# 68 tensor sums and products move from GpSimd (POOL) to VectorE (DVE) in a two-block network on one core

## The chip, the cores and the metric

One core of a Trainium2 chip runs the whole program. The metric is device time in microseconds (us) for one execution. The core has TensorE (PE), which multiplies matrices from SBUF into PSUM, three engines for everything elementwise, VectorE (DVE), ScalarE (ACT) and GpSimd (POOL), and DMA queues that are fed mainly from SyncE (SP) and, for a few small transfers, from POOL. SBUF is the on-chip memory that all engines read and write, PSUM the one into which PE accumulates. An engine takes its own instructions in order and waits on semaphores for those of others.

## The reference

The input is one sequence of 256 tokens with 1024 channels, and it passes through two blocks of two layers each.

```python
# first block, layer 0
z = modulate(rmsnorm(x)) @ w_in
x = x + gt1 * concat(hyena_mixer(z), neighborhood_attention(q, k, v, k_ctx, v_ctx, rpb)) @ w_mix_out
x = x + gt2 * swiglu(modulate(rmsnorm(x)))
# layer 1
x = x + gt1 * fourier_mix(modulate(rmsnorm(x))) @ w_fourier
x = x + gt2 * moe_swiglu(...)          # 8 experts, the best 2 of each token
# second block, layer 0
x = x + g1 * retention_mixer(h, pos)   # q and k are rotated by cos and sin of the position
x = x + g2 * conv_ffn(h)
# layer 1
x = x + g1 * s5_mixer(h)               # a complex linear recurrence over the tokens
x = x + g2 * conv_ffn(h)
return rms_norm(x) * final_norm_g
```

The recurrence of the S5 mixer is s(l) = a * s(l-1) + bu(l), with complex a for each of 64 groups and 64 states, and y = Re(C s) + d * u. Matmuls are computed in nearly full fp32 precision: each weight and each activation is split into a high part (a copy in a rounded format) and a low part (the rest), and the products high x high, high x low and low x high are summed.

## The kernel before, in words

The program is written as a sequence of stages ("segments"): the mixer's input projection with the hyena filters, the attention with its output projection, the feed-forward, the Fourier mixer with the routing, the experts, retention, the first convolutional feed-forward (conv 0), S5, conv 1 and the final norm. Within a segment, calls such as `V.tensor_mul` (DVE), `A.activation` (ACT), `G.tensor_add` (POOL) and `S.matmuls` (PE) are only recorded (class `Sched`, `record`). At the end of a segment `flush` puts them in order by list scheduling: it keeps a clock for each engine, gives each operation a cost by `cost` (a POOL sum or product of n elements a partition 0.15 + 0.0021 n us, one on DVE 0.07 + 0.00104 n us), and issues next what can start first. The order on each engine is therefore made by this planner and is redone within each segment when an operation changes its engine. Nothing moves from one segment to another.

All non-matmul instructions come from one line of the recorder, L364 in the profile, and all matmuls from L376, so the profile is read by the names of tiles. The names that matter:

- `wh`, `wl`: the high part (ACT) and the low part (DVE) of a weight tile `w`, made as weights arrive; PE needs both. `hh`/`hl`, `gh`/`gl`, `mwh` are the same for activations and expert weights.
- `w<-w,cb`: a conditioning product (ada), a row sum on DVE over a 128x1024 weight tile; `mods` collects them.
- Hyena filters (`filters`): spectra `K`, 128x512. To the first two pieces of each spectrum the skip vector is added on POOL.
- Attention (`bias`): a bias tile is loaded by DMA through the tensor `Rd`, and the mask is added to it on POOL (`bias<-bias,bias`, 128x1024). DVE then adds a part of it to the scores in PSUM (`ps_sc<-ps_sc,bias`), takes the row maximum (`nm`), and makes a diagonal matrix `dg` of the reciprocal sums, with which PE scales and transposes the probabilities.
- Routing (`route`): DVE finds the best two experts and the slots of each token in a long chain of small instructions, up to the selection matrix `oh` which PE multiplies by the tokens `tok`. `tok` has a high part (ACT) and a low part (POOL).
- Retention (`rotate`): `rqk` is raw * cos (DVE), `rt` is raw * sin (POOL), and DVE combines both.
- S5 constants (`s5_products`, `cmul`): twelve complex-product pieces 128x512 (`s5aB`, `t`, `s5C`) on POOL, issued during conv 0, and four products `s5dd` (32x256) ahead of the loop.
- S5 loop (`s5`): eight chunks of 4 state tiles. For each chunk ACT makes sine and cosine (`sc`) of the phases in `s5f`, writes the decay factors over `s5f`, and spreads the input over `s5um`; PE makes `ps_bu` (two tiles of 128x512). DVE multiplies these by cosine and sine (`a`, `b`: four products that read PSUM), POOL adds them in two instructions (`a<-a,b`), DVE scans both halves along the tokens (`a<-s5f,a`, a tensor_tensor_scan), and four products turn the state back: two on DVE (`a<-a,sc`, `b<-a,sc`) and two on POOL (`a<-a,sc`, `b<-a,sc`). PE reduces them to `ps_y`, ACT copies that into `s5f`. Behind the last chunk the gated output projection (glu) begins: `s5g` is its input, `yn` the gelu.

The loop's elementwise buffers (`pw.tile`) rotate, so ACT's `sc` of a later chunk waits until the last product of an earlier one has read the buffer.

Of the kernel before, what the change touches and what calls it, by code (L numbers as in the profile page):

```python
# [9 lines left out]
F32 = mybir.dt.float32  # L10
# [3 lines left out]
OP = mybir.AluOpType  # L14
# [5 lines left out]
L = 256  # L20
# [281 lines left out]
class Sched:  # L302
    XLAT = 0.08

    def __init__(self, tc):
        self.tc, nc = tc, tc.nc
        self.direct = False
        self.bw = 360e3
        self.ops = []
        self.V = Queue(self, "DVE", nc.vector)  # L310
        self.A = Queue(self, "ACT", nc.scalar)
        self.G = Queue(self, "POOL", nc.gpsimd)
        self.T = Queue(self, "PE", nc.tensor)
        self.Q = Queue(self, "SP", nc.sync)
        self.table = None
        self.lead = 0
# [69 lines left out]
    def add(self, op, ins, outs):  # L386
        op.idx = len(self.ops)
        op.key = (op.idx - self.lead, op.idx)
        deps = {}
        op.bufs = []  # L390
        for w, vs in ((False, ins), (True, outs)):
            for v in vs:
                if not isinstance(v, View):
                    continue
                b = v.buf
                s = (0, 128, 0, 4096) if b.psum else v.span()
                keep = []
                for (o, s2, w2) in b.log:
                    hit = s[0] < s2[1] and s2[0] < s[1] and s[2] < s2[3] and s2[2] < s[3]
                    if hit and (w or w2) and o is not op:  # L400
                        deps[o.idx] = o
                    covered = w and s[0] <= s2[0] and s2[1] <= s[1] and s[2] <= s2[2] and s2[3] <= s[3]
                    if not (covered and o is not op):
                        keep.append((o, s2, w2))
                keep.append((op, s, w))
                b.log = keep
                if b not in op.bufs:
                    op.bufs.append(b)
        op.deps = list(deps.values())
        self.ops.append(op)  # L410

    def flush(self):
# [146 lines left out]
class Net:  # L559
# [337 lines left out]
    def filters(self, p, x8, x8b, dp):  # L897

        V, A = self.V, self.A
# [10 lines left out]
        dec, skip = ds[:, 0], ds[:, 1]  # L910
# [20 lines left out]
        for o in range(2):  # L931
# [24 lines left out]
            for fch in range(4):  # L956
                ps = self.ps("hy")
                src = S if fch < 2 else Df
                self.mg(ps, [(self.dft[:, tck, fch * 128:fch * 128 + 128], src[:, tck]) for tck in range(2)])
                V.tensor_mul(K[:, fch], ps, rec)  # L960
                if fch < 2:
                    self.G.tensor_add(K[:, fch], K[:, fch], skip[:, o])
                V.memset(K[0:1, 2], 0.0)
            ps = self.ps("hy")
            self.mg(ps[0:1, :], [(self.dft[:, tck, 256:257], S[:, tck]) for tck in range(2)])
# [138 lines left out]
    def bias(self, t, hc4, c, mask):  # L1104
        o = 2048 * hc4 + 128 * c
        self.Q.dma_start(t, self.Rd.raw(lambda v: bass.AP(tensor=v.tensor, offset=v.offset + o,
                                                          ap=[[1, 128], [512, 4], [1, L]])))
        self.G.tensor_tensor(t, t, mask[:, c:c + 1].bcast(4, L), OP.add)
        return t

    def stack_heads(self, t, d, hc4, parts):
# [569 lines left out]
    def route(self, pr):  # L1681
# [114 lines left out]
        V.tensor_tensor(eq, oh[1], pw[:, :, 2:3].bcast(2, NE), OP.mult)  # L1796
        V.tensor_add(gate, gate, eq)
        pick(slice(0, 6))
        tk = pr.tile([128, 2, 2, 512], F32, name="rT", tag="fyh")
        for t in range(2):  # L1800
            for q in range(2):
                s, v = slice(q * 512, q * 512 + 512), tk[:, t, q]
                V.scalar_tensor_tensor(v, turned[2 * t + q], r[:, t:t + 1], bt[:, q], op0=OP.mult, op1=OP.add)
                A.activation(mo["tok"][:, 0, t, s], v, AF.Copy)
                self.G.tensor_sub(mo["tok"][:, 1, t, s], v, mo["tok"][:, 0, t, s].bitcast(F32))

    def gather(self, x, tags):
        mo, V = self.mo, self.V
# [75 lines left out]
    def retention(self):  # L1884
        I, V, A, G = self.I, self.V, self.A, self.G
        with self.segment("ret", dict(mm=4, st=1, o=2, tp=1), pools=(1, 2)) as (p, po):
# [9 lines left out]
            def rotate(c, ps):  # L1896
# [5 lines left out]
                if c % 2:  # L1902
                    d = qk[t][:, j]
                    t1 = po.tile([128, 2, L], F32, name="rt1", tag="rb")
                    V.tensor_mul(d, raw, cn.fold(1, L).bcast(2, L))
                    G.tensor_mul(t1, raw, sn.fold(1, L).bcast(2, L))
                    V.tensor_sub(d[:, 0], d[:, 0], t1[:, 1])
                    V.tensor_add(d[:, 1], d[:, 1], t1[:, 0])

# [157 lines left out]
    def s5_products(self, p):  # L2067
# [2 lines left out]
        self.Q.dma_start(B, self.I["s5_bc"][:, 0:2])  # L2070
        self.Q.dma_start(C, self.I["s5_bc"][:, 2:4])
        t = p.tile([128, 2, 32, 16], F32, name="t5")
        self.cmul(self.G, t, aB, B, (ar, ai))
        self.cmul(self.G, t, C, C, (fr, fi))
        self.s5BC = B, C, aB

    def s5_fill(self, n=1):
# [11 lines left out]
    def s5(self):  # L2089
# [8 lines left out]
        with self.segment("s5", dict(mm=2, bu=4, y=2), pools=(1, 2)) as (p, pw):  # L2098
# [27 lines left out]
            DB, DD = [p.tile([128, 8, 32], F32, name=n) for n in ("s5db", "s5dd")]  # L2126
            quads = [slice(32 * q, 32 * q + 32) for q in range(4)]
            for q in range(4):
                G.tensor_tensor(DD[quads[q]], self.ident[quads[q], quads[q]].fold(1, 32).bcast(8, 32),
                                dsk[quads[q]].fold(8, 1).bcast(8, 32), OP.mult)  # L2130
            for c2 in range(4):
                ps = self.ps("bu")
# [19 lines left out]
            for c in range(8):  # L2152
# [28 lines left out]
                for r in range(2):  # L2181
                    V.tensor_mul(a1[:, r], bu[r].fold(4, H), sc[:, 1])
                    V.tensor_mul(b1[:, r], bu[r].fold(4, H), sc[:, 0])
                G.tensor_add(w[:, 0], a1[:, 0], b1[:, 1])
                G.tensor_sub(w[:, 1], a1[:, 1], b1[:, 0])
                for r in range(2):
                    V.tensor_tensor_scan(w[:, r].fold(4 * H), f4.fold(4 * H), w[:, r].fold(4 * H), 0.0, OP.mult, OP.add)
                a2 = pw.tile([128, 2, 4, H], F32, name="a25")
                V.tensor_mul(a2[:, 0], w[:, 0], sc[:, 1])
                G.tensor_mul(a2[:, 1], w[:, 1], sc[:, 1])  # L2190
                V.scalar_tensor_tensor(b2[:, 1], w[:, 1], -1.0, sc[:, 0], op0=OP.mult, op1=OP.mult)
                G.tensor_mul(b2[:, 0], w[:, 0], sc[:, 0])
                py = self.ps("y")
                terms = ((0, a2, 0), (0, b2, 1), (1, b2, 0), (1, a2, 1))
                self.S.matmuls([(py[quads[q], H:2 * H], DD[:, c], um[:, 1, q], True, False) for q in range(4)]
# [81 lines left out]
```

## Time and profile before

| | |
|---|---|
| three runs | 2335.9, 2336.37 and 2342.92 us, median 2336.37 |
| the profiled execution | 2340.57 us, its span (first to last instruction) 2338.8 |
| ACT busy | 981.6 us (42%), 1722 instructions |
| POOL busy | 135.3 us (6%), 116 instructions |
| DMA | 651.66 MB, mean 279 GB/s |
| mean granted TensorE clock | 0.966 |

The busy shares are means over stages that are limited by different engines. POOL's sums and products stand in six places: the filters and the first bias tiles (up to 195 us), attention (195 to 262), routing (around 572), rotation (1542 to 1590), S5 constants (1790 to 1812) and the S5 stage (1970 to 2072). A stage is read from its own window: an engine that is busy for nearly all of a window while the others wait for it is what that window costs. Two neighbouring instructions of DVE overlap a little in the records (the next starts some 0.08 us before the end of the one before), so a sum of durations is slightly more than the time that they take in a row.

### The profile page before, as it was taken

The numbers are of one execution on the slowest core, as the hardware profiler recorded it, in microseconds if no ns is written. First come the engines' busy times: TensorE is split into PE (matmuls) and PEld (weight loads), VectorE is DVE, ScalarE is ACT, GpSimd is POOL, SyncE is SP. The second block draws the span as 40 slices with busy tenths as digits, with TensorE's granted clock in tenths as the row PEclk, the third lists the DMA queues.
The fourth block names the chain that finished last, engine by engine and source line by source line (L and its number), as shares of the span: only waits on it lengthen the run. The fifth ranks groups of instructions, "written<-read, shape, count | busy, mean of one in ns | idle before, by whom it ended". The sixth has DMA issues, their size and how long they took to land. (4 is left out here: it accounts for less than half of the span.)

```text
span 2338.8 us, 40671 instructions
## 1 busy us (share of the span) xinstructions
PE 2189.4 (94%) x16402; PEld 1599.2 (68%) x16402; DVE 1504.7 (64%) x2734; ACT 981.6 (42%) x1722; POOL 135.3 (6%) x116
## 2 busy tenths in 40 slices
PE   7998999986999999999999999899998998779998
PEld 4787889976544444454444444389998998468997
DVE  6886889875433343454444444388969998968864
ACT  4434654453222332232323332153656756436553
POOL 0013000000000000000000000010003001520000
PEclk9998999998999999999999999899999999889999
DMA  8577379965599999988989999638645685115742
GB/s 305 186 248 189 136 299 360 323 239 223 223 391 388 399 401 420 408 327 359 420 332 419 398 420 420 238 127 327 252 178 218 222 294 225 71 56 188 262 160 93
DMA packets 103868, 651.66 MB, mean 279 GB/s; under 512 B 14087, under 2 KB 20520, under 8 KB 31160
## 3 DMA queue, kind: packets, MB, share of 16 engines
q1 hardware_dynamic: 100216, 644.26, 71.2%
q0 software_dynamic: 3456, 4.72, 1.2%
q8 instruction: 131, 2.15, 0.4%
q14 instruction: 65, 0.53, 0.1%
HBM read 644.71 MB, written 4.23 MB: 277 GB/s over the span
## 5 line engine op out<-in xcount | busy, mean ns | idle before, releaser
L364 DVE TENSOR_TENSOR wl<-w,wh 128x1024 fp32r<-128x1024 f32 (+1 forms) x356 | 399.0, 1141 | 69.4 <-ACT wh L364 69.1
L376 PE MATMUL ps_mm<-hh,wh 128*128 128x256 f32 (+1 forms) x1472 | 430.8, 293 | 11.3 <-ACT hh L364 5.6
L364 ACT ACTIVATE wh<-w 128x1024 fp32r<-128x1024 f32 (+1 forms) x356 | 338.3, 979 | 236.7 <-PE ps_mm L376 173.2
L376 PE MATMUL ps_mm<-hl,wh 128*128 128x256 f32 (+1 forms) x1472 | 422.0, 287 | 5.8 <-DVE hl L364 5.7
L376 PE MATMUL ps_mm<-hh,wl 128*128 128x256 f32 (+1 forms) x1472 | 420.0, 285 | 5.5 <-DVE wl L364 5.5
L376 PE MATMUL ps_a<-w,xg 128*32 128x256 f32 (+1 forms) x3136 | 367.9, 452 | 3.9 <-DMA w<-in_moe_w 2.4
L364 DVE TENSOR_TENSOR mwh<-w,mwh 128x512 fp32r<-128x512 f32 x336 | 226.2, 689 | 124.2 <-ACT mwh L364 71.5
L364 ACT ACTIVATE mwh<-w 128x512 fp32r<-128x512 f32 x336 | 206.6, 629 | 233.3 <-PE ps_h L376 181.2
L376 PEld LDWEIGHTS ps_mm<-hh,wh 128*128 128x128 f32 x1472 | 283.1, 192 | 21.4 <-ACT hh L364 7.9
L376 PEld LDWEIGHTS ps_mm<-hl,wh 128*128 128x128 f32 x1472 | 283.3, 192 | 10.9 <-DVE hl L364 8.6
L376 PEld LDWEIGHTS ps_mm<-hh,wl 128*128 128x128 f32 x1472 | 284.2, 193 | 6.5 <-DVE wl L364 6.4
L376 PEld LDWEIGHTS ps_a<-w,xg 128*32 128x32 f32 (+1 forms) x3136 | 115.3, 118 | 160.5 <-issue 119.1
L364 DVE SCALAR_TENSOR_TENSOR w<-w,cb 128x1024 f32<-128x1024 f32 x176 | 213.4, 1233 | 6.2 <-DMA w<-in_ada_w 5.8
L376 PE MATMUL ps_h<-mwh,xs 128*128 128x512 f32 x672 | 192.9, 416 | 0.0
L376 PE MATMUL ps_a<-w,gt 128*32 128x256 f32 (+1 forms) x1568 | 183.7, 450 | 8.4 <-DVE gt L364 8.4
L376 PEld LDWEIGHTS ps_h<-mwh,xs 128*128 128x128 f32 x672 | 116.1, 189 | 61.4 <-issue 36.2
L364 ACT ACTIVATE gg<-ps_a 64x256 f32<-64x256 f32 (+1 forms) x63 | 29.8, 473 | 288.2 <-PE ps_a L376 288.2
L376 PE MATMUL ps_mm<-gh,wh 128*128 128x256 f32 x528 | 149.4, 283 | 0.0
L376 PE MATMUL ps_mm<-gh,wl 128*128 128x256 f32 x528 | 148.8, 282 | 0.2 <-DVE wl L364 0.2
L376 PE MATMUL ps_mm<-gl,wh 128*128 128x256 f32 x528 | 148.5, 281 | 0.0
L376 PEld LDWEIGHTS ps_a<-w,gt 128*32 128x32 f32 (+1 forms) x1568 | 58.4, 117 | 102.3 <-issue 63.1
L364 DVE TENSOR_TENSOR gg<-gg,ps_a 64x256 f32<-64x256 f32 (+1 forms) x63 | 33.8, 537 | 107.7 <-ACT gg L364 107.1
(454 smaller groups left out, 3491.9 us busy)
## 6 DMA issues: line engine op xcount, KB each, us to landing
w<-in_moe_w SPq DMA_DIRECT2D x336, 1024.0 KB, 10.9
w<-in_ada_w SPq DMA_DIRECT2D x88, 1024.0 KB, 6.9
w<-in_cf_up SPq DMA_DIRECT2D x44, 1024.0 KB, 5.0
w<-in_ret_in SPq DMA_DIRECT2D x24, 1024.0 KB, 4.9
w<-in_ffn_up SPq DMA_DIRECT2D x22, 1024.0 KB, 7.1
w<-in_cf_dn SPq DMA_DIRECT2D x32, 704.0 KB, 5.3
w<-in_w_in SPq DMA_DIRECT2D x12, 1024.0 KB, 7.3
w<-in_ffn_dn SPq DMA_DIRECT2D x16, 704.0 KB, 5.7
```

Source lines behind the costliest of these rows:

```text
L364: op.fn = lambda: getattr(obj, m)(*[_real(a) for a in args], **{k: _real(v) for k, v in kw.items()})
L376: mm(_real(o), _real(a), _real(b), start=st, stop=sp, skip_group_check=True)
```

## The change

Every sum, difference and product on tensors that POOL did is given to DVE, unchanged in shape and operands: 4 additions to `K`, 8 bias sums, 4 low parts of `tok`, 8 rotation products, 12 pieces of the S5 constants, 4 products `s5dd` and, in the S5 loop, 32 (16 sums, 8 + 8 products). POOL keeps its memsets and its DMAs. For the low parts of `tok` the planner also gets a dependency (`behind`), so that they are issued behind the first part of the routing's chain.

```diff
@@ Sched
+        self.behind = []
...
-        op.deps = list(deps.values())
+        op.deps = list(deps.values()) + [o for o in self.behind if o.idx not in deps]
@@ filters
                 if fch < 2:
-                    self.G.tensor_add(K[:, fch], K[:, fch], skip[:, o])
+                    V.tensor_add(K[:, fch], K[:, fch], skip[:, o])
@@ bias
-        self.G.tensor_tensor(t, t, mask[:, c:c + 1].bcast(4, L), OP.add)
+        self.V.tensor_tensor(t, t, mask[:, c:c + 1].bcast(4, L), OP.add)
@@ route
         pick(slice(0, 6))
+        last = [o for o in self.S.ops if o.eng == "DVE"][-1:]
...
                 A.activation(mo["tok"][:, 0, t, s], v, AF.Copy)
-                self.G.tensor_sub(mo["tok"][:, 1, t, s], v, mo["tok"][:, 0, t, s].bitcast(F32))
+                self.S.behind = last
+                V.tensor_sub(mo["tok"][:, 1, t, s], v, mo["tok"][:, 0, t, s].bitcast(F32))
+                self.S.behind = []
@@ rotate
                     V.tensor_mul(d, raw, cn.fold(1, L).bcast(2, L))
-                    G.tensor_mul(t1, raw, sn.fold(1, L).bcast(2, L))
+                    V.tensor_mul(t1, raw, sn.fold(1, L).bcast(2, L))
@@ s5_products
-        self.cmul(self.G, t, aB, B, (ar, ai))
-        self.cmul(self.G, t, C, C, (fr, fi))
+        self.cmul(self.V, t, aB, B, (ar, ai))
+        self.cmul(self.V, t, C, C, (fr, fi))
@@ s5
             for q in range(4):
-                G.tensor_tensor(DD[quads[q]], ...
+                V.tensor_tensor(DD[quads[q]], ...
...
                 for r in range(2):
                     V.tensor_mul(a1[:, r], bu[r].fold(4, H), sc[:, 1])
                     V.tensor_mul(b1[:, r], bu[r].fold(4, H), sc[:, 0])
-                G.tensor_add(w[:, 0], a1[:, 0], b1[:, 1])
-                G.tensor_sub(w[:, 1], a1[:, 1], b1[:, 0])
+                V.tensor_add(w[:, 0], a1[:, 0], b1[:, 1])
+                V.tensor_sub(w[:, 1], a1[:, 1], b1[:, 0])
...
                 V.tensor_mul(a2[:, 0], w[:, 0], sc[:, 1])
-                G.tensor_mul(a2[:, 1], w[:, 1], sc[:, 1])
+                V.tensor_mul(a2[:, 1], w[:, 1], sc[:, 1])
                 V.scalar_tensor_tensor(b2[:, 1], w[:, 1], -1.0, sc[:, 0], op0=OP.mult, op1=OP.mult)
-                G.tensor_mul(b2[:, 0], w[:, 0], sc[:, 0])
+                V.tensor_mul(b2[:, 0], w[:, 0], sc[:, 0])
```

What the planner makes of it is seen in the order of the instructions (engine by engine, no times). In a row stand the recorder's line, the operation, the tiles it writes and reads, and the shape; "x2" stands for two in a row, and the scan is listed as SCALAR_TENSOR_TENSOR `a<-s5f,a`.

DVE in the S5 loop, before, around the second half of one chunk and the beginning of the next:

```order
L364 SCALAR_TENSOR_TENSOR a_47630<-s5f_44830,a_47630 128x512
L364 TENSOR_TENSOR a_47661<-ps_bu,sc_47604 128x512
L364 SCALAR_TENSOR_TENSOR a_47630<-s5f_44830,a_47630 128x512
L364 SCALAR_TENSOR_TENSOR b_47639<-a_47630,sc_47477 128x512
L364 TENSOR_TENSOR a_47663<-a_47630,sc_47477 128x512
L364 TENSOR_TENSOR b_47672<-ps_bu,sc_47604 128x512
L364 TENSOR_TENSOR a_47661<-ps_bu,sc_47604 128x512
L364 TENSOR_TENSOR b_47672<-ps_bu,sc_47604 128x512
L364 TENSOR_TENSOR wl<-w,wh 128x1024
L364 SCALAR_TENSOR_TENSOR a_47661<-s5f_45125,a_47661 128x512
L364 TENSOR_TENSOR a_47714<-ps_bu,sc_47698 128x512
L364 SCALAR_TENSOR_TENSOR a_47661<-s5f_45125,a_47661 128x512
```

The same place on DVE in the changed kernel:

```order
L365 SCALAR_TENSOR_TENSOR a_47628<-s5f_44830,a_47628 128x512 x2
L365 TENSOR_TENSOR a_47662<-a_47628,sc_47472 128x512 x2
L365 SCALAR_TENSOR_TENSOR b_47637<-a_47628,sc_47472 128x512
L365 TENSOR_TENSOR b_47637<-a_47628,sc_47472 128x512
L365 TENSOR_TENSOR a_47670<-ps_bu,sc_47602 128x512
L365 TENSOR_TENSOR b_47695<-ps_bu,sc_47602 128x512
L365 TENSOR_TENSOR a_47670<-ps_bu,sc_47602 128x512
L365 TENSOR_TENSOR b_47695<-ps_bu,sc_47602 128x512
L365 TENSOR_TENSOR a_47670<-a_47670,b_47695 128x512 x2
L365 SCALAR_TENSOR_TENSOR a_47670<-s5f_45125,a_47670 128x512 x2
L365 TENSOR_TENSOR a_47736<-a_47670,sc_47602 128x512 x2
```

Before, DVE works on two chunks alternately and on weight splits between them; now it does one chunk from its four PSUM products to its last product, and then the next.

DVE at the end of the S5 loop, before, from the last chunk's scans to the glu:

```order
L364 SCALAR_TENSOR_TENSOR a_48049<-s5f_46395,a_48049 128x512
L364 SCALAR_TENSOR_TENSOR b_48148<-a_48049,sc_48024 128x512
L364 TENSOR_TENSOR a_48194<-a_48049,sc_48024 128x512
L364 TENSOR_TENSOR s5g<-yn,s5g 128x256
L364 TENSOR_TENSOR hl<-mods_44049,hh 128x8x2
L364 TENSOR_TENSOR s5g<-yn,s5g 128x256
L364 TENSOR_TENSOR wl<-w,wh 128x1024
L364 TENSOR_TENSOR glus<-glus,ps_mm 128x256
```

The same place in the changed kernel:

```order
L365 SCALAR_TENSOR_TENSOR a_48130<-s5f_46738,a_48130 128x512 x2
L365 TENSOR_TENSOR a_48185<-a_48130,sc_48032 128x512 x2
L365 SCALAR_TENSOR_TENSOR b_48136<-a_48130,sc_48032 128x512
L365 TENSOR_TENSOR b_48136<-a_48130,sc_48032 128x512
L365 TENSOR_TENSOR s5g<-yn,s5g 128x256
L365 TENSOR_TENSOR wl<-w,wh 128x1024 x4
L365 TENSOR_TENSOR hl<-mods_43972,hh 128x8x2
L365 TENSOR_TENSOR s5g<-yn,s5g 128x256
```

The four weight splits `wl` that stood between the chunks now stand behind the last of them.

DVE in the attention, in the changed kernel, where the first two bias sums of this stage now stand between the softmax's instructions (before, this place had only the latter, and an ada product `w,mods<-w,cb` a few rows on):

```order
L365 TENSOR_REDUCE nm<-ps_sc 128x1
L365 TENSOR_SCALAR dg<-k_ident,nm 128x128
L365 RECIPROCAL nm<-nm 128x1
L365 TENSOR_TENSOR bias<-bias,bias_1056 128x1024
L365 TENSOR_SCALAR dg<-k_ident,nm 128x128
L365 TENSOR_TENSOR bias<-bias,bias_1056 128x1024
L365 RECIPROCAL nm<-nm 128x1
L365 TENSOR_TENSOR ps_sc<-ps_sc,bias 128x256
```

Of the eight ada products `w,mods<-w,cb` that stood in this loop ahead of the last attention output (`catl`), five are left there; the other three follow behind it.

## Rows read from the trace of the kernel before

**Rows 1.** The page: span, and busy time of each engine.
```profile
span 2338.8 us, 40671 instructions
PE 2189.4 (94%) x16402; PEld 1599.2 (68%) x16402; DVE 1504.7 (64%) x2734; ACT 981.6 (42%) x1722; POOL 135.3 (6%) x116
```

**Rows 2.** Windows: from:to, length, busy of each engine, granted clock, DMA share, GB/s.
```profile
30.00:180.00 150.00, 150.00 (x982) 115.35 (x981) 128.34 (x220) 57.15 (x94) 16.73 (x15) 1.00 0.66 230
...
195.00:262.00 67.00, 53.19 (x384) 43.29 (x383) 61.03 (x143) 44.84 (x103) 19.78 (x15) 0.87 0.61 181
562.00:590.00 28.00, 15.59 (x98) 13.82 (x94) 14.53 (x52) 9.12 (x19) 4.94 (x4) 0.70 0.36 143
590.00:1510.00 920.00, 896.67 (x6280) 426.97 (x6280) 385.19 (x738) 267.82 (x480) 0.00 (x0) 0.99 0.93 377
1542.00:1590.00 48.00, 42.06 (x331) 41.25 (x330) 47.57 (x72) 22.69 (x38) 12.96 (x8) 0.96 0.56 201
1790.00:1812.00 22.00, 17.97 (x146) 17.55 (x145) 21.59 (x27) 11.56 (x22) 17.88 (x12) 0.97 0.57 213
...
1988.50:2071.50 83.00, 58.23 (x657) 34.99 (x655) 78.79 (x76) 38.64 (x79) 47.34 (x38) 0.84 0.13 47
```

**Rows 3.** Waits in the S5 loop: us in total, times, longest.
```profile
ACT sc L364 <- DVE a L364: 32.6, 6, 8.2
...
PE ps_y L376 <- DVE a L364: 21.0, 6, 7.8
```

**Rows 4.** DVE by form, 1960 to 2090: count, busy us, mean ns, idle before.
```profile
L364 DVE TENSOR_TENSOR_SCAN a<-s5f,a 128x512 f32<-128x512 f32 x16 | 31.6, 1978 | 1.8 <-POOL a L364 1.8
L364 DVE TENSOR_TENSOR a<-a,sc 128x512 f32<-128x512 f32 x8 | 14.0, 1746 | 0.0
...
L364 DVE TENSOR_TENSOR a<-ps_bu,sc 128x512 f32<-128x512 f32 x16 | 10.6, 675 | 2.4 <-ACT sc L364 2.1 <-issue 0.3
```

**Rows 5.** DVE in time, S5 loop: start, us, instruction, idle before.
```profile
2004.66 0.66 DVE L364 TENSOR_TENSOR a<-ps_bu,sc 128x512 f32<-128x512 f32 x1
2005.25 2.01 DVE L364 TENSOR_TENSOR_SCAN a<-s5f,a 128x512 f32<-128x512 f32 x1
...
2065.51 1.21 DVE L364 TENSOR_TENSOR_SCAN a<-s5f,a 128x512 f32<-128x512 f32 x1
2066.64 0.39 DVE L364 TENSOR_TENSOR s5g<-yn,s5g 128x256 fp32r<-128x256 f32 x1
...
2074.00 0.17 DVE L364 TENSOR_TENSOR hl<-mods,hh 128x16 fp32r<-128x16 f32 x1 [2.14 <-PE ps_y L376]
```

**Rows 6.** POOL in time, at the scan of 2005.25.
```profile
2004.91 1.26 POOL L364 TENSOR_TENSOR a<-a,sc 128x512 f32<-128x512 f32 x1 [1.25 <-DVE a L364]
```

**Rows 7.** DVE by form where PE is full, 30 to 180.
```profile
L364 DVE TENSOR_TENSOR wl<-w,wh 128x1024 fp32r<-128x1024 f32 x24 | 29.0, 1217 | 0.6 <-ACT wh L364 0.6
...
L364 DVE TENSOR_TENSOR P<-P,lc 128x512 f32<-128x512 f32 x8 | 5.5, 682 | 0.0
```

**Rows 8.** DVE in time, attention.
```profile
199.30 0.28 DVE L364 TENSOR_SCALAR dg<-k_ident,nm 128x128 f32<-128x128 f32 x1
...
205.93 2.78 DVE L364 TENSOR_SCALAR dg<-k_ident,nm 128x128 f32<-128x128 f32 x1
```

**Rows 9.** POOL in time, at the dg of 205.93.
```profile
206.27 2.35 POOL L364 TENSOR_TENSOR bias<-bias,bias 128x1024 f32<-128x1024 f32 x1
```

**Rows 10.** DVE by form, attention, 195 to 262.
```profile
L364 DVE TENSOR_SCALAR dg<-k_ident,nm 128x128 f32<-128x128 f32 x31 | 16.8, 552 | 0.2
```

**Rows 11.** DVE in time, routing.
```profile
574.37 1.19 DVE L364 TENSOR_SCALAR big<-oh 128x16 f32<-128x16 f32 x1
...
577.01 0.17 DVE L364 TENSOR_TENSOR eq<-lg,mx 128x16 f32<-128x16 f32 x1
```

**Rows 12.** DVE by form, rotation, 1542 to 1590.
```profile
L364 DVE TENSOR_TENSOR rqk<-rraw,cn 128x512 f32<-128x512 f32 x8 | 7.6, 946 | 0.0
```

**Rows 13.** DVE by form, S5 constants, 1790 to 1812.
```profile
L364 DVE TENSOR_TENSOR wl<-w,wh 128x1024 fp32r<-128x1024 f32 x6 | 9.8, 1644 | 0.0
```

More of the change, by code (lines that the diff above doesn't have):

```diff
@@ L2128, in s5 @@
             for q in range(4):
-                G.tensor_tensor(DD[quads[q]], self.ident[quads[q], quads[q]].fold(1, 32).bcast(8, 32),
+                V.tensor_tensor(DD[quads[q]], self.ident[quads[q], quads[q]].fold(1, 32).bcast(8, 32),
                                 dsk[quads[q]].fold(8, 1).bcast(8, 32), OP.mult)
```

## The prediction
> **What bounds the kernel now.** I read first the page's busy times: PE works for 94% of the span, DVE for 64%, POOL for 6% [rows 1]. So a saving counts only where PE stands still. The table of windows shows where. Between 30 and 180 us PE is busy for all 150 us, and with the experts, from 590 to 1510, for 896.7 of 920: what DVE gains or loses there is hidden, and costs something only beyond the slack (DVE 128 of 150 and 385 of 920). In the other windows where POOL computes, DVE is the full engine and PE has holes: in the attention DVE 61.0 of 67 and PE idle for 13.8; in the rotation DVE 47.6 of 48, PE idle 5.9; with the S5 constants DVE 21.6 of 22, PE idle 4.0; in the S5 loop DVE 78.8 of 83, PE idle 24.8 [rows 2]. In the routing both have holes, since it is one chain of short dependent instructions. In the loop the waits say who is late: ACT's `sc` waited 32.6 us for DVE's products, PE's `ps_y` 21.0 [rows 3]. The loop therefore costs what DVE takes for it.
>
> Next I looked at what DVE's time in these windows is made of. The same scan takes 1.21 us at 2065.51 and 2.01 at 2005.25, and its mean over 16 is 1.978; the product `a<-a,sc` has a mean of 1.746 [rows 4, 5], though a sum or product of this shape with both inputs in SBUF takes 0.682 where POOL is quiet [rows 7]. The long scan began at 2005.25 and ended at 2007.26. POOL's product ran from 2004.91 to 2006.17 [rows 6]: the scan ended 1.09 us behind POOL's end, about one clean scan later, as if it had begun only then. In the attention the same: a `dg` of 0.28 us lasted from 205.93 to 208.71, and POOL's bias sum ended at 208.62 [rows 8, 9]. Products that read PSUM do not show it (mean 0.675, and the one at 2004.66 has 0.66 beside that POOL product) [rows 4 to 6]. So I read the trace thus: while POOL works on tensors, a DVE instruction that reads only SBUF stands still.
>
> The Trainium skill has this as a rule ("SBUF — State Buffer", section "Who interferes with whom"): DVE shares one pair of SBUF ports with GpSimd, whoever has it holds it for the whole instruction, and a DVE instruction with two SBUF inputs contends with a GpSimd instruction that reads SBUF. The trace agrees (1.21 us against 2.01).
>
> **The S5 loop, the largest term.** Neighbours on DVE overlap by 0.08 us (2065.51 + 1.21 = 2066.72, and the next starts at 2066.64) [rows 5], so an instruction takes its duration less 0.08: a 512-wide sum or product 0.682 - 0.08 = 0.60 [rows 7], one from PSUM likewise 0.60, a scan 1.13. The order shows what a chunk will hold: four PSUM products, two sums, two scans, four products back. That is 10 x 0.60 + 2 x 1.13 = 8.26 us, for eight chunks 66.1. Seven `s5g` by 0.32 (the one of 0.39) [rows 5] add 2.2. The loop becomes 68.3 us instead of 83.0 [rows 2], 14.7 less.
>
> The sum from the other side: added are 32 x 0.60 = 19.2. Given back are 16 x (1.978 - 1.21) = 12.3 on the scans, 8 x (1.746 - 0.682) = 8.5 on the products [rows 4, 5, 7], 4.2 of DVE's idle time in the window [rows 2], and the four weight splits that leave the loop, 4 x (1.217 - 0.08) = 4.5 [rows 7], together 29.5. That makes 10.3; the other 4 must come from other stretched instructions of the loop (the splits and `s5g` themselves).
>
> The four splits are not gone. They stand behind the last chunk now, ahead of `hl`. There DVE was idle for 2.14 us before [rows 5], so 4.5 - 2.1 = 2.4 us come back at the tail. **The stage saves 14.7 - 2.4 = 12.3; I take 12.** From below: if ACT or PE takes the lead, 3 (see the rivals). From above: 15, with a free tail. The four `s5dd` ahead of the loop add about 1.4 (estimate, 4 x 0.35 from half of a 512-wide instruction) where POOL's own block others there; I count nothing, within 1 either way.
>
> **Attention.** Six bias sums, 128x1024, cost DVE 6 x (1.217 - 0.08) = 6.8, by the split of the same shape [rows 7]. Given back on the 31 `dg`: 31 x (0.552 - 0.28) = 8.4 [rows 8, 10]. Further, three ada products leave the loop for the place behind it. They have the shape of the split; at its 1.14 us each that is 3.4 less ahead of the last output of the attention. 6.8 - 8.4 - 3.4 = -5.0. Against it stands a new wait: a bias sum on DVE waits for its DMA, and behind it in the queue wait `dg`, `nm` and with them PE, where POOL waited alone before. The order puts it early, so I take 1 us of this. **-4.** Bounds: the sums all exposed, nothing given back and one ill-timed DMA, +9; all of PE's idle time but a few us of it, -10.
>
> **Rotation and S5 constants.** Eight rotation products add 8 x 0.60 = 4.8. The eight `rqk` give back 8 x (0.946 - 0.682) = 2.1 [rows 7, 12], and more lies in the others that ran meanwhile, which I can't sum by form. Between +2.7 (only `rqk` gives back) and -5.9 (PE's idle time there) I take **-1**. For the constants, the twelve pieces cost 12 x 0.60 = 7.2 on DVE, but the planner puts two of them where POOL's twelve stood and spreads the others over the rest of conv 0, where PE was the later engine again; 1.2 is in the way. The six splits alone give back 6 x (1.644 - 1.217) = 2.6 [rows 7, 13], and no more than PE's 4.0 idle us can be won. Between +3 and -4 I take **-2**. If the spread pieces lie in DVE's way after all, 6.0 of cost is at stake.
>
> **Routing, filters, first bias sums.** Routing has four low parts (4 x 0.60 = 2.4) in the chain ahead of `oh`; the chain gets back about 1.0 on `big` (1.19 where its neighbour `eq` of the same shape takes 0.17) [rows 11], and another 1.0 or more on the instruction behind it. I take 0, between +2.4 and -2.5. Four sums into `K` and two bias sums come where PE is busy for 150 of 150 us [rows 2]: 4 x 0.60 + 2 x 1.14 = 4.7 us of DVE work into 22 us of its slack, 0, within 2.
>
> **Sum:** -12 - 4 - 1 - 2 = -19. The profiled execution took 2340.57 us, 1.8 more than its span, so 2321.6 under the profiler. It lay 4.2 above the median of the runs, 2336.37; taken from that, **2317**.
>
> **Rivals.**
> - *The stretch is not given back.* Then the long scans are long by themselves, and DVE, full in four windows, gets 68 more instructions: S5 19.2 less its 4.2 of idle time, +15; attention +6.8, rotation +4.8, constants +7.2, routing +2.4: +36, 2373 us, slower. It decides at the loop: 24 scans and products there must give back (19.2 - 4.2) / 24 = 0.63 us each on the mean, otherwise it is longer than before. Against it speaks the clean scan of 1.21 in the same loop with the same shape, and that the blocked one ends with POOL; for it, that just one clean scan was found in the rows. The Trainium skill ("Perfetto Trace Analysis", section "Optimizing Scalar/DVE Operations") says that with a saturated DVE it may make sense to offload work even to GPSIMD, which would speak for before; it adds that the shared port may spoil it, and the rows of the scan are of that kind.
> - *ACT or PE takes over the loop.* Before, DVE worked on two chunks alternately; now one chunk is a closed row, and the `ps_y` of a chunk, the `sc` two chunks on and PE's `ps_bu` follow only when its last product is done. PE's 58.2 us in the window, an eighth of which is 7.3 a chunk [rows 2], lie near the 8.26 of DVE, and the granted clock was 0.84 there, a mix of the two levels of 1.2 and 2.4 GHz. If waits put 1.2 us on each chunk, 9.6 of the 14.7 are gone: 2336.4 - 9 = 2327. For it: PE's idle time before each `ps_y`. Against: eight chunks' worth of idle PE time, and PE's products for later chunks can be made ahead.
> - *Only the S5 loop pays.* A late bias DMA stops DVE in the attention, the rotation gives back only what its row shows, and the constants nothing: 2336.4 - 12 = 2324; with +5 in the attention 2329. What speaks for it is that earlier stages are followed by the experts, where DMA is busy for 0.93 of the time [rows 2] and may have been the pace; against it, PE's 896.7 of 920.
> - *The change doesn't do what it says* I exclude: in the order, POOL has only memsets and DMAs left.
>
> **Chances.** Forecast 0.66 (its own range 2306 to 2325), ACT or PE takes over 0.14, only S5 pays 0.12, stretch not given back or given back by half (2345 to 2373) 0.08. What a measurement of this kernel can tell from no change is about 0.3%, 7 us: faster means below 2329.4. Of the second case 7 in 10, of the third 6 in 10 lie below it, so faster 0.66 + 0.10 + 0.07 = 0.83, same 0.09, slower 0.08. The range is 2302 to 2334: up to the worse ends of the second and third case, down to a free tail, -6 in the attention and -4 in the rotation; the slower case and a little at either end stay outside.
>
> **What would show it.** Right: the 16 scans at 1.21 on the mean, `a<-a,sc` x16 near 0.68, the loop from the first `ps_bu` product to the last product some 66 to 70 us, `dg` near 0.28 throughout, no long `rqk`. The tail is right if `hl` waits behind four splits. The second rival shows as idle time of DVE before `a<-ps_bu,sc`, waiting for ACT `sc` or PE `ps_bu`, of over 1 us a chunk; the third as DVE waiting for `Rd` and unchanged lengths of the rotation and constants windows; the first as scans still near 2 us without POOL. I am wrong if the loop takes more than 75 us, or if the attention ends later than before.

## The result: 1.2% faster, and the profile after

The changed kernel took 2313.41 us (median of 6 runs, 2310.48 to 2315.66), the kernel before 2341.66 in the runs beside it (2335.9 to 2353.76). The ratio is 0.9876 (95% interval 0.9859 to 0.9892), 29 us less. Timed once more on another occasion it was 0.9872 (0.9851 to 0.9893). I had forecast 19 us less. The first three runs of before had a lower median (2336.37) than all of them, so ratios and traces are compared from here on.

The page of the changed kernel, the rows that answer to [rows 1]:

```profile
span 2309.1 us, 40635 instructions
PE 2181.6 (94%) x16402; PEld 1592.8 (69%) x16402; DVE 1489.3 (64%) x2806; ACT 983.7 (43%) x1724; POOL 22.1 (1%) x44
```

DVE has taken over 113 us of POOL's work and is busy for 15 us less than before: 72 more records, and the others shorter. To find the places I compared, in the two traces, the start of the k-th of the 16402 matmuls, whose order is the same at the boundaries of the segments. The time between two such marks is the length of a stage. Here it stands for five traces (us; marks at the first instruction, at matmul 1000, 1600, 4000, 9900, 11800, 12100, 12400, 13100, 13640 and 14600, and at the last matmul):

```
                      before  after  after again  att. bias only  constants only
input, filters         174.8  174.6    173.4         174.7           173.8
attention               95.1   81.3     83.8          81.7            93.7
ffn to routing         348.0  351.3    350.8         349.3           345.8
experts                849.4  843.0    846.4         844.6           851.5
retention              284.4  284.3    284.4         286.1           286.1
conv 0 up               42.8   43.2     43.2          43.8            43.8
S5 constants            41.5   35.6     35.6          42.1            35.6
conv 0 down             83.1   83.1     83.1          83.1            83.1
ahead of the S5 loop    63.9   68.0     65.6          64.0            66.9
S5 loop and glu        117.1  105.9    103.9         115.5           115.4
conv 1, norm           228.8  228.7    228.7         228.8           228.7
```

The gain lies in the attention (11 to 14 us), the S5 stage (11 to 13) and the constants (6, of which 2 to 4 are lost again ahead of the S5 loop). Retention as a whole is unchanged; what goes on inside it is shown with the rotation below. The experts vary from 843 to 851 us between executions of kernels whose edits lie elsewhere, so the 6 us there are no effect of the change. Their length goes with TensorE's granted clock, which has two levels in these traces, 2.4 GHz (1.00) and 1.2 GHz (0.50): it stood at the lower one for 3.4 us of the 843.0, for 13.7 of the 849.4 and for 20.5 of the 851.5. The 3 us that the stretch from the feed-forward to the routing lost are no clear effect either: the six kernels below that add something to the whole change take 347.6 to 351.4 us there.

Windows of the changed kernel (from:to, length, busy of each engine, granted clock, DMA share, GB/s), the answer to [rows 2]: the attention, then the loop from its first PSUM product to its last product.

```profile
195.00:250.00 55.00, 49.29 (x402) 41.73 (x401) 51.28 (x142) 44.74 (x104) 4.82 (x9) 0.94 0.62 174
...
1970.90:2039.60 68.70, 50.09 (x644) 26.53 (x642) 68.14 (x106) 36.95 (x77) 0.63 (x6) 0.92 0.07 28
```

The loop lasts 68.7 us (82.9 before), DVE is busy for 68.1 of it. DVE by form around it (1969 to 2046: count, busy us, mean ns, idle before), the answer to [rows 4]:

```profile
L365 DVE TENSOR_TENSOR_SCAN a<-s5f,a 128x512 f32<-128x512 f32 x16 | 18.8, 1223 | 0.0
L365 DVE TENSOR_TENSOR a<-ps_bu,sc 128x512 f32<-128x512 f32 x16 | 11.1, 696 | 0.6 <-PE ps_bu L377 0.6
...
L365 DVE TENSOR_TENSOR a<-a,b 128x512 f32<-128x512 f32 x16 | 10.4, 698 | 0.0
L365 DVE TENSOR_TENSOR a<-a,sc 128x512 f32<-128x512 f32 x16 | 10.3, 691 | 0.0
```

All 16 scans have the length of the one clean scan of before, and DVE waited once, 0.6 us. The tail, DVE in time (start, us, instruction, idle before), the answer to [rows 5]:

```profile
2038.86 0.72 DVE L365 TENSOR_TENSOR b<-a,sc 128x512 f32<-128x512 f32 x1
2039.46 0.46 DVE L365 TENSOR_TENSOR s5g<-yn,s5g 128x256 fp32r<-128x256 f32 x1
2039.80 4.66 DVE L365 TENSOR_TENSOR wl<-w,wh 128x1024 fp32r<-128x1024 f32 x4
2044.33 0.21 DVE L365 TENSOR_TENSOR hl<-mods,hh 128x16 fp32r<-128x16 f32 x1
```

`hl` stands 4.8 us behind the last product, where it stood 2.5 behind it before.

DVE by form in the attention (195 to 250), the answer to [rows 10]:

```profile
L365 DVE TENSOR_SCALAR dg<-k_ident,nm 128x128 f32<-128x128 f32 x31 | 8.5, 279 | 0.0
L365 DVE TENSOR_TENSOR bias<-bias,bias 128x1024 f32<-128x1024 f32 x6 | 7.3, 1218 | 1.0 <-DMA bias<-Rd 1.0
...
L365 DVE SCALAR_TENSOR_TENSOR w<-w,cb 128x1024 f32<-128x1024 f32 x2 | 2.4, 1212 | 0.0
L365 DVE TENSOR_TENSOR wl<-w,wh 128x1024 fp32r<-128x1024 f32 x2 | 2.4, 1212 | 0.0
```

### The profile page after: what moved, and what is told of

Read it like the earlier page. It is cut to its first block, busy times and chain, and to the rows that moved or that the text cites. A ratio compares the mean times of both kernels' runs of the same rounds, so it can differ in the third digit from the quotient of the medians.

```text
span 2309.1 us, 40635 instructions
## 1 busy us (share of the span) xinstructions
PE 2181.6 (94%) x16402; PEld 1592.8 (69%) x16402; DVE 1489.3 (64%) x2806; ACT 983.7 (43%) x1724; POOL 22.1 (1%) x44
## 5 line engine op out<-in xcount | busy, mean ns | idle before, releaser
L377 PE MATMUL ps_mm<-hh,wh 128*128 128x256 f32 (+1 forms) x1472 | 431.6, 293 | 12.7 <-ACT hh L365 6.4
L377 PEld LDWEIGHTS ps_mm<-hh,wh 128*128 128x128 f32 x1472 | 283.0, 192 | 23.0 <-ACT hh L365 10.3
```

Source lines behind the costliest of these rows:

```text
L377: mm(_real(o), _real(a), _real(b), start=st, stop=sp, skip_group_check=True)
```

## The experiments

**The change in parts.** Five kernels make one part of the change each: only the lines of that part have `V.` for `G.`, in the fifth with the planner's dependency for `tok`.

```diff
# s5_only                                   # bias_only
-G.tensor_add(w[:, 0], ...)  (and 4 more)   -self.G.tensor_tensor(t, t, mask..., OP.add)
+V.tensor_add(w[:, 0], ...)                 +self.V.tensor_tensor(t, t, mask..., OP.add)
# const_only                                # rot_only
-self.cmul(self.G, t, aB, B, (ar, ai))      -G.tensor_mul(t1, raw, sn...)
+self.cmul(self.V, t, aB, B, (ar, ai))      +V.tensor_mul(t1, raw, sn...)
# tokk_only
-self.G.tensor_add(K..., skip...)  and  self.G.tensor_sub(mo["tok"][:, 1, t, s], ...)
+V.tensor_add(K..., skip...)       and  V.tensor_sub(mo["tok"][:, 1, t, s], ...)
```

S5 only: 

> Only the S5 loop's 32 sums and products and the four s5dd go to DVE; all else as before. If the stages add up independently: the loop from its first PSUM product to its last product takes 68 to 70 us (82.9 before, 68.6 with the whole change), PE's lead over before stays at 0 until the S5 stage and is 9 to 12 us behind it, so 2326 to 2333 where before gives about 2338. If the S5 gain needed the other edits (the planner's order of the stage, or what the constants leave on DVE), the lead behind the stage is under 6 us. If the stretch is only one of several causes, the scans stay above 1.5 us on the mean; otherwise they are 1.22.

Ratio 0.9956 (0.9941 to 0.9972), 10 us less. Loop 68.0 us, scans 1.205 on the mean, S5 stage 103.6. The loop's edit stands alone and gives all of its gain.

Bias sums only: 

> Only the eight bias sums go to DVE. With the whole change PE led by 0.2 us at 195 us and by 14.0 at the end of the attention, where I had forecast 4. If all of that comes from the bias sums: lead 12 to 15 us behind the attention, dg 0.28 us on the mean (0.55 before), 2324 to 2329. If the lead partly came from what stands ahead of it (K, order in the filters), under 9 us. Through the experts the lead should stay as it is; if it grows there by some 3 to 6 us as it did with the whole change, an earlier start changes how loads and matmuls meet in the experts; if not, that growth was a matter of the single execution.

Ratio 0.9942 (0.992 to 0.9964), 14 us less. The attention takes 81.7 us, `dg` 0.277 on the mean. So all of the gain that I had sized at 4 belongs to this one line. PE's lead over before grew by 3.7 us around the experts' first part here too. It did so in all five kernels that make one part of the change (by 2.4 to 3.7), so it is a feature of the execution of before to which they are compared: there the clock stood at its lower level for 3.4 us of that part, in the five not at all.

Constants only: 

> Only the twelve pieces of the S5 constants go to DVE. With the whole change PE won 5.9 us between 1785 and 1815 us and lost 1.7 and then some 2 to 3 us between 1905 and 1985. If both belong to this edit (the pieces spread over conv 0 push ada products behind it, where DVE is late): +5 to 6 us lead behind the first stretch, 2 to 5 of it lost before the S5 loop, net -1 to -4 us. If the later loss comes from the S5 edit instead: the 5 to 6 us stay, 2331 to 2333 against 2338.

Ratio 0.998 (0.9963 to 0.9996), 5 us less (1 to 9). The stage of the constants is 35.6 us as in the whole change, and the stretch ahead of the loop 66.9 (63.9 before, 64.2 with S5 alone). The later loss thus belongs to this edit. (The whole change lost 4.1 and 1.7 us there in its two traces; the longer one has the clock at its lower level for 6.8 us, the others for 3.4.) PE's waits in 1890 to 1990 (us in total, times, longest) show two on DVE that before has none of:

```profile
PE ps_mm L376 <- DVE wl L364: 1.6, 1, 1.6
PE ps_mm L376 <- DVE w L364: 0.7, 1, 0.7
```

Rotation only: 

> Only the eight rotation products go to DVE. With the whole change PE's lead grew by 5 us from 1530 to 1655 us and fell by 5.2 around 1670, net 0. If the fall belongs to this edit (DVE work that was pushed back comes due there): the same up and down here, net within 1 us. If the fall was another edit's or a matter of one execution: a net lead of 3 to 5 us. My forecast was 1. The long rqk should be gone in any case (mean 0.69 instead of 0.95).

Ratio 0.9999 (0.9983 to 1.0015): the kernel's time does not move. The rise and the fall are both there. Windows of the same matmuls (10100 to 10600 with the rotation, then 11000 to 11200), first before, then with the rotation's products on DVE:

```profile
1528.40:1599.00 70.60, 64.66 (x501) 62.31 (x500) 64.52 (x100) 32.36 (x52) 12.96 (x8) 0.98 0.54 194
...
1652.70:1678.20 25.50, 25.50 (x203) 23.96 (x201) 23.49 (x47) 20.55 (x35) 0.00 (x0) 1.00 0.53 197
```
```profile
1519.60:1585.80 66.20, 63.76 (x501) 60.93 (x500) 61.23 (x103) 33.29 (x53) 0.00 (x0) 1.00 0.53 189
...
1638.60:1667.80 29.20, 27.33 (x202) 24.11 (x201) 28.02 (x59) 23.23 (x39) 0.00 (x0) 1.00 0.62 225
```

The rotation takes 4.4 us less (66.2 with the whole change too), and no `rqk<-rraw,cn` is longer than 0.69. The later stretch takes 3.7 us more here and 5.2 with the whole change: DVE has 59 instructions there instead of 47, which I take for the work that was pushed back, and PE, which had waited for nothing there, waits for `wl` (0.9 us), `roT` (0.7) and `wh` (0.3). Retention as a whole took 281.4 us in this trace, 284.3 and 284.4 with the whole change and 284.4 before.

Filters and tokens only: 

> Only the four sums into K and the four low parts of tok (with their dependency) go to DVE, the rest as before: what is left of the change when bias sums, rotation, constants and S5 are taken out. Forecast 0, since the filters lie under a full PE and the routing's chain gives as much as it takes: within 3 us of before, 2336 to 2344. If the routing's tail is exposed, PE's lead falls by 1 to 2.4 us around 570 us.

Ratio 1.0004 (0.9991 to 1.0017), and the stage with the routing's tail (matmul 3700 to 4000) 56.3 us (56.8 before, 58.1 in both traces of the whole change). The five parts add up to -10.3 - 13.6 - 4.7 - 0.2 + 0.9 = -28 us at 2342, the whole is -29 to -30.

**Is it POOL's reading of SBUF, or the handoffs and the order?** Two kernels give POOL work in the S5 loop for which nobody waits; DVE's order stays that of the changed kernel through all of its 2806 records.

```diff
+            def shadow(n):                      # called behind the PSUM products and behind the scans
+                self.S.behind = [o for o in self.S.ops if o.eng == "DVE"][-1:]
+                for j in range(n):
+                    G.tensor_add(B[:, 0].fold(512), bw[:, 0:2].fold(512), bw[:, 2:4].fold(512))   # s5_shadow, n = 2
+                    G.memset(B.fold(1024), 0.0)                                                   # s5_memset, n = 3
+                self.S.behind = []
```

Sums: 

> The changed kernel, and POOL also adds two constant 128x512 tiles of SBUF into a tile that nobody reads, twice behind the last PSUM product and twice behind the second scan of each chunk, as many and as large as the sums that it lost. Nothing waits for POOL, and DVE's order is unchanged. If a POOL instruction that reads SBUF stops DVE's SBUF-only instructions: 32 POOL sums of 1.3 to 1.5 us, scans and products that meet them 1.7 to 2.5 us, and the loop of 68.6 us grows by 20 to 40 us. If before was slow through its waits between the engines and its order: no growth beyond 2 us.

Ratio 0.9975 (0.9957 to 0.9993): nearly the whole gain of the change is gone. The loop took 93.2 us. DVE and POOL by form (1975 to 2080):

```profile
L365 DVE TENSOR_TENSOR_SCAN a<-s5f,a 128x512 f32<-128x512 f32 x16 | 32.3, 2055 | 0.0
L365 DVE TENSOR_TENSOR a<-a,b 128x512 f32<-128x512 f32 x16 | 18.5, 1196 | 0.0
...
L365 DVE TENSOR_TENSOR a<-ps_bu,sc 128x512 f32<-128x512 f32 x16 | 10.8, 675 | 0.0
```
```profile
L365 POOL TENSOR_TENSOR s5B<-k_s_b 128x512 f32<-128x512 f32 x32 | 53.4, 1669 | 2.0
```

The scans are at 2.055 again and the sums at 1.196, the PSUM products at 0.675. The expectation was wrong on where POOL would work: `behind` orders the planner alone and makes no wait on the chip, so the four sums of a chunk ran in one go. POOL's 53.4 us cost the loop 24.5.

Memsets: 

> The changed kernel, and at the same two places of each chunk POOL fills a dead tile of 128x1024 with zeros, three times each (0.95 us each, 46 us in all, as long as the sums it lost): it writes SBUF and reads nothing. If only reads of SBUF by POOL stop DVE: loop 68.6 us within 1.5, scans 1.22. If any POOL access to SBUF stops it: growth of 20 us or more, as with the sums.

Ratio 0.9844 (0.981 to 0.9877), that of the changed kernel. The loop is 68.0 us, with POOL at work for 46 of them:

```profile
L365 DVE TENSOR_TENSOR_SCAN a<-s5f,a 128x512 f32<-128x512 f32 x16 | 18.6, 1197 | 0.0
```
```profile
L365 POOL MEMSET s5B<- 128x1024 f32 x48 | 45.7, 952 | 2.4
```

So it is not POOL's activity or its writes, as these memsets make them, but instructions that read SBUF.

**How much of the attention is this?** Two kernels add the like to the attention of the changed kernel: 12 sums of 128x480 or 6 of 128x960 (written in bf16 for want of space).

```diff
         self.V.tensor_tensor(t, t, mask[:, c:c + 1].bcast(4, L), OP.add)
+        if hc4:
+            m = mask[:, c:c + 1, 0:240].bcast(4, 240)          # att_wide; att_shadow: two of bcast(2, 240)
+            self.G.tensor_tensor(self.shadow, m, m, OP.add)
```

Short: 

> The changed kernel, and POOL adds 128x480 tiles of SBUF into a tile that nobody reads, two behind each of the six bias sums in the attention (12 in all, about 14 us, as long as what it lost). DVE's order is that of the changed kernel, with the three ada products behind the loop. If the lead of 13.8 us of the attention is stretch given back: 9 to 14 us are lost again, dg back to 0.5 us on the mean. If it is mostly the order (ada products moved out, scores' chain sooner): under 5 us lost. In between, the shares are what it says.

Ratio 0.9856 (0.9825 to 0.9888), attention 82.7 us, `dg` only 0.341: nothing lost. POOL took 14.7 us in two bursts, but `dg` waited at most 0.7 us for one of the short instructions, so this run doesn't answer the question.

Wide: 

> The changed kernel, and POOL makes one 128x960 sum of SBUF tiles into a tile that nobody reads behind each of the six bias sums of the attention, about as long as one bias sum on POOL (2.3 us). Shadows of half the size gave back only 3 us of stretch, and cost PE 1.5 us or less. If the length of a single POOL instruction decides (a dg that meets it waits up to 2.3 us): dg 0.4 to 0.55 us on the mean, PE 4 to 12 us later behind the attention. If it is still under 2 us, most of the 13.6 us that the bias sums give comes from the order of the softmax and the ada products, or from when POOL's sums stood, not from the length.

Ratio 0.9898 (0.9876 to 0.9919) against 0.9872 beside it; the attention took 87.4 us. DVE in time, DVE by form (195 to 255) and POOL in time:

```profile
204.80 2.23 DVE L365 TENSOR_SCALAR dg<-k_ident,nm 128x128 f32<-128x128 f32 x1
```
```profile
L365 DVE TENSOR_SCALAR dg<-k_ident,nm 128x128 f32<-128x128 f32 x31 | 15.9, 518 | 0.0
```
```profile
205.11 7.63 POOL L365 TENSOR_TENSOR sh<-bias 128x960 bf16<-128x960 f32 x3
```

With nearly all of `dg`'s stretch back (15.9 of 16.8 us), the attention is 4 to 6 us longer than in the two traces of the changed kernel, and still 8 us shorter than before. The rest is therefore not `dg`. (The clock stood at its lower level for 13.7 us of it, for 6.8 in those two and for 17.1 before, so these 4 to 6 us hold what PE lost by that as well.)

**Can POOL work beside the PSUM products?** Since these are not disturbed, one product of the chunks 0 to 6 was given back to POOL.

```diff
-                V.tensor_mul(b2[:, 0], w[:, 0], sc[:, 0])
+                if c < 7:
+                    V.tensor_copy(b2[:, 0, 0, 0:1], b2[:, 1, 0, 0:1])   # s5_beside2; s5_beside: behind = the last DVE op
+                    G.tensor_mul(b2[:, 0], w[:, 0], sc[:, 0])
+                else:
+                    V.tensor_mul(b2[:, 0], w[:, 0], sc[:, 0])
```

First: 

> The changed kernel, but in chunks 0 to 6 one product (b<-a,sc) goes back to POOL with a dependency on DVE's last SBUF product of the chunk, so that POOL works while DVE does the four PSUM products of the next chunk (2.4 us). If PSUM products are not stopped by POOL: the loop shrinks by 7 x 0.6 = 4 us, to 64 to 65, and the kernel is 2 to 4 us faster than the changed one. If POOL's 1.3 to 1.6 us reach into the sums, or ps_y waits for it: no gain or up to 4 us slower than the changed kernel.

Ratio 0.9844 (0.9808 to 0.9881), loop 69.8 us, with three of the four weight splits (3.6 us) back in it. The planner's dependency did not hold POOL back here either. DVE and POOL in time, chunk 1 (at 1991) and chunk 2 (at 2001):

```profile
1991.61 2.33 DVE L365 TENSOR_TENSOR a<-a,sc 128x512 f32<-128x512 f32 x2
...
2001.51 1.27 DVE L365 TENSOR_TENSOR a<-a,sc 128x512 f32<-128x512 f32 x2
2002.69 0.68 DVE L365 SCALAR_TENSOR_TENSOR b<-a,sc 128x512 f32<-128x512 f32 x1
```
```profile
1991.77 1.62 POOL L365 TENSOR_TENSOR b<-a,sc 128x512 f32<-128x512 f32 x1 [4.52 <-DVE a L365]
...
2001.77 2.74 POOL L365 TENSOR_TENSOR b<-a,sc 128x512 f32<-128x512 f32 x1 [5.27 <-DVE a L365]
```

In chunk 1 DVE's pair takes 1.06 us more than in chunk 2. In chunk 2 it is POOL whose product takes 2.74, where it needs 1.27 alone (shown below): it got its turn about when the pair and the product behind it were through (2001.77 + 2.74 - 1.27 = 2003.24). So either engine can be the one that waits. In both chunks POOL's product starts behind the pair's first product and ahead of its second, by the records, 0.16 and 0.26 us after the pair's start; which of the two will wait can't be read from the order of the starts alone.

With a true wait: 

> As the kernel with one product of chunks 0 to 6 back on POOL, but with a true wait: POOL's product is issued behind a one-column copy on DVE that reads the chunk's last SBUF product, so it starts beside the PSUM products of the next chunk and no longer beside a<-a,sc. If PSUM products and POOL don't disturb each other: a<-a,sc 0.68 in all chunks, POOL's product 1.6 us, 7 x (0.60 - 0.1) = 3.5 us off DVE's row, of which the splits that the planner now puts into the loop take back the part that they save at the tail: 2 to 4 us faster than the changed kernel. If the copy's handoff, or ps_y waiting for POOL, costs as much: within 1.5 us of it.

Ratio 0.985 (0.983 to 0.987), 2310.17 us, beside 0.9872 (2312.06) for the changed kernel: 2 us, inside both intervals. POOL in time, and DVE by form in the loop (1978.2 to 2049.26):

```profile
2004.03 1.27 POOL L365 TENSOR_TENSOR b<-a,sc 128x512 f32<-128x512 f32 x1 [6.80 <-DVE b L365]
```
```profile
L365 DVE TENSOR_TENSOR wl<-w,wh 128x1024 fp32r<-128x1024 f32 x4 | 6.3, 1605 | 0.0
```

`a<-a,sc` took 0.68 in all chunks and POOL's product mostly 1.27 us, so these two do not meet any more. But the loop took 71.1 us, since the planner put the four splits back into it, and now two of them met POOL's product (2.0 us each instead of 1.22), together 6.3 us, and an ada product (1.2) came in too. The stage took 103.8, as with the changed kernel. Whether it is the best version can't be told.

## Why the prediction was right, and which terms were off

**The reading of the stretch** held where it was put to use: DVE instructions with two inputs in SBUF stand still while POOL reads SBUF (`s5_shadow`), they don't with memsets (`s5_memset`), and PSUM products never did. With that the first rival, the one on the slower side, is out. As I had worded it, for any DVE instruction that reads only SBUF, it was too wide. In before, DVE and POOL in time:

```profile
230.85 0.17 DVE L364 RECIPROCAL nm<-nm 128x1 f32<-128x1 f32 x1
230.93 2.67 DVE L364 SCALAR_TENSOR_TENSOR w<-w,cb 128x1024 f32<-128x1024 f32 x1
```
```profile
230.16 5.64 POOL L364 TENSOR_TENSOR bias<-bias,bias 128x1024 f32<-128x1024 f32 x2 [5.06 <-DVE dg L364]
```

Beside the same sums of POOL the reciprocal, with one input, keeps its length (mean 0.154 us), and the product with two takes 2.67 us instead of 1.22. The Trainium skill ("SBUF — State Buffer", section "Who interferes with whom") says further that the order of issue decides which of the two engines blocks, and that a GpSimd instruction that only writes SBUF does not contend with a two-input DVE instruction. These runs agree with the second: a loop of 68.0 us beside 45.7 us of memsets. On the first they show only that either engine can be the one that waits; by the starts in the records the order does not decide, since the `dg` of 205.93 waited for a sum that starts 0.34 us behind it [rows 8, 9].

**S5, forecast -12, measured -11 to -13.** The loop was forecast at 68.3 us and took 68.7 and 68.5 with the whole change and 68.0 with S5 alone. The price of each DVE instruction came from clean rows elsewhere in the same trace, and the planner's order gave the count (six `s5g` stand in the loop, I had counted seven). The 4 us that the second sum left to other stretched instructions are in before's rows: the four splits took 1.558 us on the mean, seven `s5g` 0.662 and eight `b<-a,sc` 0.787 (clean 1.217, 0.39 and 0.68), together 4.1 us of stretch. The tail came out as forecast: 2.4 us later counted, 4.8 - 2.5 = 2.3 measured. ACT or PE did not take over: DVE waited 0.6 us in the loop.

**Attention, forecast -4, measured -11 to -14: the mis-sized term, beyond its own bound of -10.** The same piece of the program, from the end of DVE's `catl<-z,cath` to its last `catl<-ps_pv,cath`, before, after, and in `att_wide` (from:to, length, busy of each engine, granted clock, DMA share, GB/s):

```profile
195.60:269.20 73.60, 59.79 (x459) 49.24 (x459) 65.98 (x157) 46.51 (x106) 19.78 (x15) 0.88 0.63 194
```
```profile
195.34:256.25 60.91, 55.20 (x467) 47.06 (x467) 57.19 (x155) 46.12 (x106) 4.82 (x9) 0.94 0.66 195
```
```profile
194.79:261.81 67.02, 58.55 (x468) 50.01 (x468) 64.63 (x155) 46.49 (x106) 17.73 (x15) 0.90 0.58 177
```

DVE by form in the piece, before and after:

```profile
L364 DVE TENSOR_TENSOR ps_sc<-ps_sc,bias 128x256 f32<-128x256 f32 x31 | 12.3, 418 | 2.6 <-PE ps_sc L376 2.6
L364 DVE SCALAR_TENSOR_TENSOR w<-w,cb 128x1024 f32<-128x1024 f32 x8 | 11.0, 1399 | 1.6 <-DMA w<-in_ada_w 1.6
```
```profile
L365 DVE TENSOR_TENSOR ps_sc<-ps_sc,bias 128x256 f32<-128x256 f32 x31 | 12.3, 423 | 0.0
L365 DVE SCALAR_TENSOR_TENSOR w<-w,cb 128x1024 f32<-128x1024 f32 x5 | 6.0, 1217 | 0.0
```

The three prices of the forecast were right: `dg` gave back 8.3 us (8.4 forecast), the six sums took 6.8 in a row (6.8), three ada products left (3.4). Two things were wrong. I left out stretch on DVE's other instructions: one ada product of 2.67 us and one `mods` sum of 1.65, where clean ones take 1.22 and 0.15, 3.0 together. And the wait had the wrong sign. I had put +1 for the bias DMA, and it came (1.0 us, 2.0 in the second trace); but all of DVE's idle time in the piece fell from 7.6 to 3.7 us (6.2 in the second trace), because waits for PE's scores (2.6), for an ada weight's DMA (1.6) and for ACT's `cath` (0.8) went away. The sum: -8.3 + 6.8 - 3.4 - 3.0 - 3.9 = -11.8, of 12.7 measured in the piece.

In `att_wide`, with `dg`'s stretch back, DVE works for nearly as long as before (64.6 us, 66.0), yet the piece is 6.6 us shorter, and DVE's idle time in it 2.4 us instead of 7.6. So what remains beside `dg`'s share of 4 to 6 us is for the most part waits that are gone. What took them away stays open: nobody waits for POOL's bias sums any more, the ada products stand elsewhere, and the clock stood at its lower level for less time. No run separates these.

**Constants, forecast -2, measured -6, and +2 to +4 later.** I had limited the gain by PE's 4.0 us of idle time. But the granted clock was 0.97 in the stretch. In equal pieces of the program (457 to 458 matmuls), PE before and after:

```profile
1780.00:1840.00 60.00, 55.97 (x458) 55.55 (x457) 57.76 (x94) 39.16 (x74) 17.88 (x12) 0.97 0.67 240
```
```profile
1763.00:1817.00 54.00, 54.00 (x457) 54.00 (x457) 50.30 (x95) 37.40 (x70) 0.00 (x0) 1.00 0.74 267
```

PE's busy time itself fell by 2.0 us, from 55.97 to 54.00, when its idle holes went and the granted clock rose from 0.97 to 1.00. In before the low stretch begins where the holes end (PE idled for 4.0 us between 1790 and 1812):

```profile
1810.70:1814.10 3.40, 2.90 (x13) 2.91 (x14) 3.40 (x7) 2.17 (x6) 0.00 (x0) 0.50 0.20 43
```

At 0.50, which is 1.2 GHz, 3.4 us hold 1.7 us of work at 2.4 GHz (an estimate from the two levels), most of the 2.0. So closing the holes gave more than their own length, and PE's idle time was no upper bound. The attention has a like rise (0.88 to 0.94). The cost of spreading the pieces, which I had named at up to 6 us, came to 2 to 4, with PE waiting for DVE's `wl` and `w` ahead of the S5 loop. The gain lies beyond my bound of -4, and a cost that I had not put into the sum takes part of it back: that the net of -2 to -4 fits the forecast is in part luck.

**Rotation (-1), routing, filters and first bias sums (0)**: each within what the runs can tell from nothing (0.9999 and 1.0004). The rotation's own matmuls took 4.4 us less, well beyond the -1, and 4 to 5 us were lost again some 70 us later, where DVE had more to do than before, a term that I did not have; that the two cancel is luck. The case "only the S5 loop pays" is out, by the bias sums.

**The total.** Forecast were 19 us less, measured 29: the mechanism was right, and most of the missing 10 are the attention's. That the forecast time of 2317 us lies within 4 us of 2313.41 is in part luck, since it was taken from a median of before (2336.37) that is 5.3 us lower than that of the six runs.

## What to carry to other kernels

Before work is offloaded to POOL, look at what DVE does meanwhile: beside PSUM-reading instructions it costs nothing, beside those with two inputs in SBUF a POOL instruction that reads SBUF can take up to its own length out of DVE (24.5 us of 53.4 in `s5_shadow`). Price a moved instruction by clean rows of the same shape, take the count from the order, and sum over all that DVE does in the stage, its neighbours' stretch, what leaves it and where that goes included. Don't take PE's idle time for the most that can be won where its granted clock is below 1.

## What was not expected of the hardware

- The stop works both ways: a POOL product that takes 1.27 us alone took 2.74 beside three DVE products, and 1.62 where DVE was the one that waited.
- POOL's memsets, 45.7 us of them in a loop of 68.0, cost DVE nothing.
- A short DVE instruction on one tile and a column of scalars (`dg`, 128x128, 0.28 us) is stopped as well, for 2 us and more (2.78 [rows 8]).
- Closing PE's holes with the S5 constants gave 4.0 us of idle time and about 2 us of clock.
